# A two-block transformer kernel, its instructions ordered by the other model of time

## The chip, the cores and the metric

One core of one Trainium2 chip. The metric is the device time of one execution in microseconds (us), taken as the median of the runs shown. The engines are PE (TensorE, with its weight loads apart as PEld), DVE (VectorE), ACT (ScalarE), POOL (GpSimd) and SP (SyncE, whose queue here issues all plain loads and stores).

## The reference

Two blocks run one after the other on a sequence of 1024 rows of width 1024, all in fp32. What the change bears on most is cut out here:

```python
def first_block(...):                       # retention part of the mixer
    scores = jnp.einsum('bnihd,bnjhd->bnhij', qc, kc) * decay_in
    y_in = jnp.einsum('bnhij,bnjhe->bnihe', scores, vc)
    kv = jnp.einsum('bnjhd,bnjhe,hj->nbhde', kc, vc, zeta)
...
def second_block(...):
    q, k, v, bg, cg, hv = jnp.split(h @ w_in[l], SPLIT_POINTS, axis=-1)
    att = windowed_attention(q, k, v, k_c, v_c, sink[l])
    conv = short_conv_mixer(bg, cg, hv, conv_w[l])      # bg * conv3(cg * hv)
    x = x + gt1 * (jnp.concatenate([att, conv], axis=-1) @ w_out[l])
    x = x + gt2 * expert_choice_ffn(h2, w_router[l], w_gate[l], w_up[l], w_down[l])
```

Block 1 is a mixer (a 31-tap depthwise convolution beside an 8-head retention in chunks), cross attention over 256 memory rows and a squared-ReLU MLP of width 4096. Block 2 is a windowed attention (8 query heads on 2 key heads; every query sees 256 context keys, the keys at most 128 positions away, and a sink) beside a gated 3-tap convolution, then a mixture of 16 experts, each of which picks its 128 best tokens, and a last norm. A vector of modulations, 6 x 1024 from a matrix of 1024 x 6144, shifts, scales and gates block 2.

## The kernel before

**Products.** Every fp32 product is three matmuls on high and low parts (`mm3`, L139 to L141). Weights come in units of 128x1024 (512 KB, `raw`, L123) and are split by ACT (high part, L114) and DVE (low part, L115) into a ring of five tiles (four during the attention). A block of 128x512 outputs over 1024 inputs is 24 matmuls of 512 columns into one bank of PSUM.

**Order.** The kernel's text issues instructions for one engine after the other; the tile context reorders them before the program is built. It keeps a heap of instructions that are ready, with the position in the text as priority (`tc.high_priority(offset=n)` moves a piece n places ahead), and a model of time that says when an engine and its operands are free. What it writes is one fixed list for each engine, and an engine works through its list in order: an instruction that waits holds back all behind it. The SP queue is such a list too.

**Retention** (block 1, L445 to L524). `retention(t)` is called for 8 tiles of 128 rows: transposes of q and k (`qkT`, L453), copies by ACT (L455, L458), scores (`sc`, L462), decay by DVE, `yin` (L471), copies by ACT (L474), transposes (`yT`, L477), and the state's part (`yx`, L484; `kv`, L499). It is a chain that goes back and forth between PE, ACT and DVE. Later in the text stand the norm and transposes of the convolution's result (`yc` L565, `ptz` L578) and the keys and values of the memory (`km`, `vm`), which depend on nothing of it, then the output product `wo`.

**Attention** (block 2, L926 to L1003). `attention(t)` is called for 8 tiles of 128 queries, t = 0 to 7, and inside for two key heads `kv`, each with four query heads in two pairs:

```python
        p = B(PTB(), "q2T")                                   # L932, transposes L934
        ...
            act.activation(qT[0:64, :, r, :], src, AF.Copy)   # L938, then DVE L939
        ...
                    s2 = ps[0].tile([128, 1024], F32, tag=f"D{jj}", bufs=1, name=nm("s2"))
        ...
                        dve.tensor_reduce(mx, sc, axis=AX.X, op=OP.max)
        ...
                    act.activation(P[:, :256 + nl], sc, AF.Exp, bias=nmx[:, jj:jj + 1], scale=0.125,
        ...
            for kb in range(nkb):
                p = B(PTB(), "P2T")                           # transposes L984
                ...
                evac_split(ph, pl_, p)                        # ACT L201, DVE L202
```

The scores of a head (L956 to L961, five matmuls) go to one of two double banks (D0 and D1, one for each head of a pair); DVE takes the maximum (L964, L966), ACT the exponential (L968) with its row sum. After a pair the row sums are finished (L971 to L975) and P is scaled (L978). Then for each block of 128 keys (five; four in tiles 0 and 7) the four heads' P are transposed into one of two banks (`PTB`), split by ACT and DVE into `P2h` and `P2l`, and multiplied by the values (`o`, L992 to L995). `cor` (L998) and `att` (L1000) close a key head. `q2T` takes a bank of the same pair as the `P2T`.

**Gated convolution** (L1009 to L1037). It stands behind the attention in the text, but depends on nothing of it. For each of four channel groups it has six blocks of 24 matmuls (`cg`, `hv`, `cg`, `hv`, `bg`, `bg`), 24 blocks or 576 matmuls in all, into one bank, read by ACT (L1020) and DVE (L1024, L1035), with the taps on DVE (L1026 to L1028).

**After both** (`mixed`, L1071 to L1117) the attention's and the convolution's results are loaded back from HBM (`mf`), split into `m` (L114, L115, 512 columns) and multiplied by the output weights (`wo`); `lb` (L1054) is a small product ahead of them. Then follow the router, the top-k of 16 rounds on DVE (L1136 to L1139), and the experts.

The change touches `build` alone.

Of the kernel before, what the change touches and what calls it, by code (L numbers as in the profile page):

```python
# [1354 lines left out]
def build(shapes, stop=None, dbg=None):  # L1355
    import concourse.bacc as bacc
    nc = bacc.Bacc("TRN2", target_bir_lowering=False, num_devices=1)
    d = {n: nc.dram_tensor(n, s, dt, kind="ExternalInput").ap() for n, (s, dt) in shapes.items()}
    out = nc.dram_tensor("out_0_dram", (S, D), F32, kind="ExternalOutput").ap()
    dd = {n: nc.dram_tensor(n, s, F32, kind="ExternalOutput").ap() for n, s in (dbg or {}).items()}  # L1360
    with tile.TileContext(nc) as tc:
        tile_kernel(tc, d, out, stop=stop, dbg=dd)
    return nc

# [7 lines left out]
```

## Time and profile before

| what | value |
|---|---|
| median of 3 runs | 2562.68 us (2561.54 to 2565.68) |
| profiled execution, its own time | 2566.32 us |
| its span | 2564.5 us |
| PE, PEld busy | 95%, 77% of the span |
| DVE, ACT, POOL busy | 69%, 45%, 2% |
| mean granted clock of TensorE | 0.979 |
| chain that ended last, by engine | PE 69%, DMA 12%, DVE 12%, ACT 3% |
| HBM traffic | 172 GB/s over the span |

A busy share is a sum over stages with different limits. The chain is followed back from the last instruction to whatever released it. The granted clock has two levels, 1.2 and 2.4 GHz; a PEclk of 1.00 is the upper one all the time, 0.50 the lower. Rows of PE overlap, since matmuls are pipelined: the distance from one start to the next says more than the duration.

### The profile page before, as it was taken

The page shows a single profiled execution, that of the slowest core. Times are in us where ns is not written, and L with a number is a line of the kernel's source. Part 1 is how long each engine was busy: PE and PEld are TensorE (multiplying, and loading weights), DVE is VectorE, ACT ScalarE, POOL GpSimd, SP SyncE. Part 2 cuts the span into 40 slices and gives each one's busy share as a digit, 9 for nine tenths or more (in the row PEclk, how much of TensorE's full clock was granted, in tenths as well). Part 3 has the DMA queues.
Part 4 walks back from the last instruction along what each step waited for, and adds up shares of the span by engine and source line. Part 5 has one row for each costly group of instructions (what it writes and reads, how often), then busy time and mean ns, then how long its engine had stood idle before and what let it go on. Part 6 is the DMA issues. An engine that isn't in the chain of part 4 may idle for free.

```text
span 2564.5 us, 31365 instructions
## 1 busy us (share of the span) xinstructions
PE 2428.0 (95%) x11441; PEld 1968.6 (77%) x11441; DVE 1781.0 (69%) x3158; ACT 1165.1 (45%) x1782; POOL 56.4 (2%) x37
## 2 busy tenths in 40 slices
PE   7999899999999999999999999998983999999995
PEld 6887678888878888888888777776872888888774
DVE  6999883655577555333336758776557999999887
ACT  6113652544442122112215635554332888887775
POOL 0000000000000000000000000000000100011100
PEclk9999999999999999999999999999996999999998
DMA  5233445424443344211112221125672999999994
GB/s 192 86 125 119 162 160 196 141 96 164 135 156 123 124 141 155 65 42 47 58 50 78 91 74 50 38 65 166 209 281 97 385 395 390 391 389 385 359 374 156
DMA packets 138619, 442.85 MB, mean 173 GB/s; under 512 B 15680, under 2 KB 20320, under 8 KB 138464
## 3 DMA queue, kind: packets, MB, share of 16 engines
q1 hardware_dynamic: 133712, 423.54, 46.3%
q0 software_dynamic: 4752, 17.30, 2.7%
q8 instruction: 90, 1.47, 0.2%
q14 instruction: 65, 0.53, 0.1%
HBM read 388.34 MB, written 52.45 MB: 172 GB/s over the span
## 4 chain that ended last, share of the span: by engine, by line
PE 69%; DMA 12%; DVE 12%; ACT 3%; issue 2%; SPq 0%; DVEq 0%; POOLq 0%; ACTq 0%
DMA wada<-w_ada 7%; PE up L140 5%; PE up L141 4%; PE up L139 4%; PE dn L140 4%; PE dn L139 4%; PE dn L141 4%; DVE mws L738 3%; PE wo L140 3%; PE wo L139 3%; PE wo L141 3%; PE ga L140 2%; PE ga L141 2%; PE ga L139 2%; DVE w L115 2%
## 5 line engine op out<-in xcount | busy, mean ns | idle before, releaser
L114 ACT ACTIVATE w<-raw 128x1024 fp32r<-128x1024 f32 x560 | 584.4, 1058 | 754.1 <-PE dn L141 266.8
L115 DVE TENSOR_TENSOR w<-raw,w 128x1024 fp32r<-128x1024 f32 x560 | 674.1, 1223 | 188.7 <-ACT w L114 183.4
L139 PE MATMUL up<-hm,w 128*128 128x512 f32 x512 | 199.6, 390 | 0.0
L139 PE MATMUL dn<-w,uT 128*128 128x512 f32 x512 | 199.4, 390 | 0.1
L140 PE MATMUL up<-hm,w 128*128 128x512 f32 x512 | 199.4, 389 | 0.0
L141 PE MATMUL up<-hm,w 128*128 128x512 f32 x512 | 199.3, 389 | 0.0
L140 PE MATMUL dn<-w,uT 128*128 128x512 f32 x512 | 199.1, 389 | 0.0
L141 PE MATMUL dn<-w,uT 128*128 128x512 f32 x512 | 198.7, 389 | 0.0
L738 DVE CUSTOM_DVE_ANT_0 mws<-wada,crow 128x512 bf16<-128x512 f32 x128 | 88.2, 689 | 105.7 <-DMA wada<-w_ada 103.7
L773 DVE TENSOR_TENSOR acc<-dn,acc 128x512 f32<-128x512 f32 x144 | 97.9, 687 | 91.3 <-PE dn L141 91.0
L395 DVE SCALAR_TENSOR_TENSOR y<-u,small,y 128x1007 f32<-128x1007 f32 (+26 forms) x120 | 146.3, 1263 | 0.5
L139 PEld LDWEIGHTS dn<-w,uT 128*128 128x128 f32 x512 | 96.1, 188 | 20.9 <-DVE uT L758 0.4
L141 PEld LDWEIGHTS dn<-w,uT 128*128 128x128 f32 x512 | 96.0, 188 | 20.6 <-DVE uT L759 0.5
L141 PEld LDWEIGHTS up<-hm,w 128*128 128x128 f32 x512 | 96.1, 188 | 20.1
L139 PEld LDWEIGHTS up<-hm,w 128*128 128x128 f32 x512 | 96.0, 188 | 19.9 <-ACT hm L204 0.3
L140 PEld LDWEIGHTS dn<-w,uT 128*128 128x128 f32 x512 | 96.1, 188 | 19.8
L140 PEld LDWEIGHTS up<-hm,w 128*128 128x128 f32 x512 | 96.1, 188 | 19.7
L140 PE MATMUL ga<-w,x1T 128*128 128x512 f32 x256 | 102.8, 402 | 1.7 <-DVE w L115 1.7
L140 PE MATMUL dn<-w,x1T 128*128 128x512 f32 x256 | 101.6, 397 | 2.0 <-DVE w L115 2.0
L139 PE MATMUL dn<-w,x1T 128*128 128x512 f32 x256 | 102.3, 400 | 0.4 <-ACT w L114 0.4
L141 PE MATMUL ga<-w,x1T 128*128 128x512 f32 x256 | 102.3, 400 | 0.0
L140 PE MATMUL up<-w,x1T 128*128 128x512 f32 x256 | 101.7, 397 | 0.2 <-DVE w L115 0.2
(417 smaller groups left out, 5451.1 us busy)
## 6 DMA issues: line engine op xcount, KB each, us to landing
raw<-experts SPq DMA_DIRECT2D x384, 512.0 KB, 6.8
wada<-w_ada SPq DMA_DIRECT2D x48, 512.0 KB, 3.6
raw<-up_fm SPq DMA_DIRECT2D x32, 512.0 KB, 4.3
raw<-down_tm SPq DMA_DIRECT2D x32, 512.0 KB, 4.4
raw<-w_out_tm SPq DMA_DIRECT2D x24, 512.0 KB, 4.4
raw<-w_in_fm SPq DMA_DIRECT2D x20, 512.0 KB, 3.8
h_d<-hx SPq DMA_DIRECT2D x32, 256.0 KB, 3.0
raw<-xq_fm SPq DMA_DIRECT2D x16, 512.0 KB, 5.2
```

Source lines behind the costliest of these rows:

```text
L114: act.activation(hi, src, AF.Copy)
L115: dve.tensor_sub(lo, src, hi.bitcast(F32))
L139: pe.matmul(out_, l[0], r[0], start=first, stop=False)
L140: pe.matmul(out_, l[0], r[1], start=False, stop=False)
L141: pe.matmul(out_, l[1], r[0], start=False, stop=last)
L395: dve.scalar_tensor_tensor(yc[:, s:], uc[:, :1024 - s], convw[:, c, 30 - s:31 - s], yc[:, s:], op0=OP.mult, op1=OP.add)
L738: dve.tensor_tensor_reduce(out=mjunk, in0=raw[:, h * 512:(h + 1) * 512], in1=crow[o, h], op0=OP.mult, op1=OP.add, scale=1.0, scalar=0.0, a ...
L773: dve.tensor_add(acc[t][:, sl], p, acc[t][:, sl])
```

## The change

One argument of the tile context is set, so that the order of every engine's list is worked out with the context's other model of time, which follows engines and loads on a time line. No instruction is written differently.

```diff
--- before.py
+++ after.py
@@ -1358,7 +1358,7 @@
-    with tile.TileContext(nc) as tc:
+    with tile.TileContext(nc, schedule_with_timeline_sim=True) as tc:
         tile_kernel(tc, d, out, stop=stop, dbg=dd)
```

The two builds have the same instructions, but for loads of ACT's function tables, 45 before and 51 now. Three places where the lists differ are shown: each row is source line, operation, output<-inputs and shape; `x4` stands for four alike. Names are those of the text with a running number.

PE, where attention tile 3 ends and tile 4 begins (`q2T_12989` is tile 4's). Before:

```order
L984 MATMUL P2T_12970<-ident,PW 128x128 x2
L984 MATMUL P2T_12970<-ident,P_2285_12916 128x128
L934 MATMUL q2T_12989<-ident,qt_12986 128x128 x4
L139 MATMUL hv_14262<-hT_1945_11462,w_14172 128x512
L140 MATMUL hv_14262<-hT_1945_11462,w_14172 128x512
L141 MATMUL hv_14262<-hT_1945_11462,w_14172 128x512
L139 MATMUL hv_14262<-hT_1948_11472,w_14172 128x512
L140 MATMUL hv_14262<-hT_1948_11472,w_14172 128x512
L992 MATMUL o_2287_12925<-P2l_12976,V_1880_11058 64x512
L993 MATMUL o_2287_12925<-P2h_12975,V_1880_11058 128x512
L141 MATMUL hv_14262<-hT_1948_11472,w_14172 128x512
L958 MATMUL s_2310_13000<-K_1873_11051,qT_2306_12988 128x384
```

Now:

```order
L984 MATMUL P2T_12970<-ident,P_2285_12916 128x128
L993 MATMUL o_2287_12925<-P2h_12964,V_1879_11057 128x512
L995 MATMUL o_2287_12925<-P2l_12965,V_1879_11057 64x512
L934 MATMUL q2T_12989<-ident,qt_12986 128x128 x4
L992 MATMUL o_2287_12925<-P2l_12976,V_1880_11058 64x512
L993 MATMUL o_2287_12925<-P2h_12975,V_1880_11058 128x512
L958 MATMUL s_2310_13000<-K_1873_11051,qT_2306_12988 128x384
L958 MATMUL s_2310_13000<-K_1874_11052,qT_2306_12988 128x384
L961 MATMUL s_2310_13000<-K2c_11055,qT_2306_12988 128x256 x2
L958 MATMUL s_2313_13011<-K_1873_11051,qT_2306_12988 128x384
L958 MATMUL s_2313_13011<-K_1874_11052,qT_2306_12988 128x384
```

Before, `hv` and `bg` matmuls of the convolution stand between the steps of every attention tile, some three blocks to a tile, and the last five blocks behind the last tile. Now all 24 blocks stand earlier, in runs of 14 to 24 matmuls from the first tile on; the last, `bg_14681`, is issued when the first key head's scores of tile 3 are out. Behind it, in the rest of tile 3 and in tiles 4 to 7, PE's list has attention alone, and `q2T` of a tile stands behind all `P2T` of the one before.

PE, retention tile 6 (`qkT_2443`), with the memory's values `vm`. Before:

```order
L139 MATMUL vm_3202<-w_3184,hP_376 128x512
L453 MATMUL qkT_2443<-ident,qr_2439 128x128 x4
L140 MATMUL vm_3202<-w_3184,hP_376 128x512
L141 MATMUL vm_3202<-w_3184,hP_376 128x512
L139 MATMUL vm_3202<-w_3184,hP_376 128x512
L140 MATMUL vm_3202<-w_3184,hP_376 128x512
L141 MATMUL vm_3202<-w_3184,hP_376 128x512
L139 MATMUL vm_3202<-w_3189,hP_386 128x512
L140 MATMUL vm_3202<-w_3189,hP_386 128x512
L141 MATMUL vm_3202<-w_3189,hP_386 128x512
L139 MATMUL vm_3202<-w_3189,hP_386 128x512
```

Now:

```order
L140 MATMUL vm_3306<-w_3275,hP_406 128x512
L141 MATMUL vm_3306<-w_3275,hP_406 128x512
L453 MATMUL qkT_2443<-ident,qr_2439 128x128 x4
L462 MATMUL sc_2453<-qbd_1396,qkT_1755 128x512
L462 MATMUL sc_2457<-qbd_1396,qkT_1755 128x512
L499 MATMUL kv_2390<-vl_2345,kz_2388 128x256 x2
L471 MATMUL yin_2462<-pf_2455,vl_2441 128x256 x2
L471 MATMUL yin_2467<-pf_2459,vl_2441 128x256 x2
L484 MATMUL yx_2478<-St_1395,qkT_1755 128x256 x2
L477 MATMUL yT_2472<-ident,yF_2461 128x128 x4
```

Before, `vm_3202` and another block stood inside tiles 6 and 7, and `vm_3278` and `vm_3306`, 48 matmuls, behind tile 7. Now all `km` and `vm` blocks stand ahead of tile 6: tiles 6 and 7 and the `ptz` behind them have nothing between, and `wo` follows.

ACT, the splits of the results loaded back (`m`), which `wo` needs. Before they stand together behind the attention:

```order
L114 ACTIVATE m_2659_14742<-mf_14739 128x512
L114 ACTIVATE m_2660_14745<-mf_14739 128x512
L114 ACTIVATE m_2662_14751<-mf_14748 128x512
L114 ACTIVATE m_2663_14754<-mf_14748 128x512
L114 ACTIVATE m_2665_14760<-mf_14757 128x512
L114 ACTIVATE m_2666_14763<-mf_14757 128x512
```

Now those of `mf_14757` and `mf_15237`, which are results of the convolution, stand in tile 5, between the copies of its `q2T` and its first exponentials:

```order
L938 ACTIVATE qT_2378_13243<-q2T_13244 64x4x128
L114 ACTIVATE m_2665_14760<-mf_14757 128x512
L998 ACTIVATE cor_13236<-o_2359_13180 64x512
L114 ACTIVATE m_2666_14763<-mf_14757 128x512
L938 ACTIVATE qT_2378_13243<-q2T_13244 64x4x128
L968 ACTIVATE P_2384_13264,y_13253<-s_2382_13255,y_13254 128x640
L114 ACTIVATE m_2755_15240<-mf_15237 128x512
L114 ACTIVATE m_2756_15243<-mf_15237 128x512
```

The same holds for DVE's half of these splits, and, in tile 6, for those of `mf_14748` (the attention's results of tiles 0 to 3). `m_2659` and `m_2660` stand behind the last tile in both: `mf_14739` lies where the attention keeps a P.

## Rows read from the trace of the kernel before

**Rows 1.** Page, part 1: busy time of each engine (share of the span) and instructions.

```profile
PE 2428.0 (95%) x11441; PEld 1968.6 (77%) x11441; DVE 1781.0 (69%) x3158; ACT 1165.1 (45%) x1782; POOL 56.4 (2%) x37
```

**Rows 2.** Windows: window, us, busy of PE, PEld, DVE, ACT, POOL (x instructions), PEclk, DMA, GB/s.

```profile
1514.60:1798.70 284.10, 272.41 (x1401) 212.22 (x1402) 208.94 (x447) 143.14 (x302) 0.00 (x0) 0.99 0.25 77
...
240.00:350.00 110.00, 100.64 (x511) 77.36 (x511) 94.60 (x306) 59.74 (x124) 0.00 (x0) 0.97 0.46 154
```

**Rows 3.** Groups of instructions, PE, 1514 to 1800 us: count, then busy us, mean ns.

```profile
L139 PE MATMUL cg<-hT,w 128*128 128x512 f32 x64 | 27.0, 422 | 2.8 <-DVE y L1035 1.1 <-ACT K L871 0.9 <-DVE u L1024 0.8
```

**Rows 4.** Timeline, PE: start us, us, instruction.

```profile
1647.33 0.34 PE L956 MATMUL s<-wmr 128*128 128x384 f32 x1
...
1648.08 0.40 PE L141 MATMUL bg<-hT,w 128*128 128x512 f32 x1
...
1651.53 0.39 PE L141 MATMUL bg<-hT,w 128*128 128x512 f32 x1
```

**Rows 5.** Groups of instructions, DVE, 1514 to 1800 us.

```profile
L202 DVE TENSOR_TENSOR P2l<-P2T,P2h 128x512 fp32r<-128x512 f32 x76 | 50.7, 686 | 24.1 <-ACT P2h L201 23.8
...
L964 DVE TENSOR_REDUCE y<-s 128x1 f32<-128x640 f32 x48 | 39.2, 822 | 7.5 <-PE s L961 6.9
...
L978 DVE TENSOR_SCALAR P<-P,y 128x640 f32<-128x640 f32 x30 | 16.0, 548 | 0.2
...
L115 DVE TENSOR_TENSOR w<-raw,w 128x1024 fp32r<-128x1024 f32 x13 | 15.8, 1219 | 7.8 <-ACT w L114 7.8
...
L939 DVE TENSOR_TENSOR qT<-q2T,qT 64x512 fp32r<-64x512 f32 x16 | 11.0, 689 | 11.7 <-ACT qT L938 11.5
...
L1000 DVE TENSOR_TENSOR att<-o,cor 64x512 f32<-64x512 f32 x16 | 10.9, 683 | 6.0 <-ACT cor L998 5.8
...
L966 DVE SCALAR_TENSOR_TENSOR y<-y,nsink 128x1 f32<-128x1 f32 x64 | 9.8, 154 | 0.2
```

**Rows 6.** Groups of instructions, ACT, 1514 to 1800 us.

```profile
L201 ACT ACTIVATE P2h<-P2T 128x512 fp32r<-128x512 f32 x76 | 43.0, 596 | 41.2 <-PE P2T L984 32.4 <-PE o L993 5.4 <-DVE PW L978 1.6
...
L968 ACT ACTIVATE P<-s,y 128x640 f32<-128x640 f32 x30 | 23.8, 795 | 24.0 <-DVE y L966 19.0 <-DVE y L975 5.0
...
L938 ACT ACTIVATE qT<-q2T 64x512 fp32r<-64x512 f32 x16 | 9.5, 592 | 11.1 <-PE q2T L934 7.3 <-DVE qT L939 3.7
...
L968 ACT ACTIVATION_READ_ACCUMULATOR P<-s,y 128x1 f32 x40 | 7.8, 195 | 0.0
```

**Rows 7.** Chain of waits, 1755 to 1800 us: start us, us, what.

```profile
1787.85 5.03 DMA mf<-at
...
1792.96 0.62 ACT m L114
...
1798.71 0.61 PE wo L139
```

**Rows 8.** Chain of waits, 285 to 304 us (retention).

```profile
293.30 0.48 ACT qkT L455
...
300.55 0.22 PE yT L477 x2
```

**Rows 9.** Windows, as rows 2, of 20 us.

```profile
700.00:720.00 20.00, 16.14 (x75) 12.82 (x74) 13.07 (x33) 16.55 (x22) 0.00 (x0) 1.00 0.85 289
...
1415.00:1435.00 20.00, 15.48 (x114) 13.57 (x112) 19.66 (x84) 15.02 (x32) 0.00 (x0) 0.99 0.42 156
```

**Rows 10.** Chain of waits, 1918 to 1970 us (top-k).

```profile
1931.00 1.20 DVE x L193
...
1932.80 1.12 DVE x L1107
```

**Rows 11.** Windows, as rows 2, of 10 us.

```profile
270.00:280.00 10.00, 6.25 (x50) 5.63 (x48) 7.14 (x27) 4.57 (x8) 0.00 (x0) 1.00 0.79 257
...
280.00:290.00 10.00, 9.81 (x43) 7.38 (x44) 7.11 (x23) 3.65 (x9) 0.00 (x0) 0.83 0.36 119
...
1510.00:1520.00 10.00, 6.99 (x23) 5.24 (x24) 2.39 (x8) 3.15 (x14) 0.00 (x0) 0.66 0.49 158
```

## What the change will do: the prediction

> **What bounds the kernel now.** I read the page's busy shares first: TensorE (PE) is busy 95% of the span, VectorE (DVE) 69%, ScalarE (ACT) 45% [rows 1]. So a new order can gain only what PE idles, 5% of the span, and can lose wherever it leaves PE without work. The windows by stage come next, for the two stages in which PE's list changes most. In the attention stretch, 1514.6 to 1798.7 us, PE is busy 272.41 of 284.10 us, DVE 208.94 and ACT 143.14; in the retention's, 240 to 350 us, PE 100.64 of 110 and DVE 94.60 [rows 2]. A reader is to see that PE is nearly full in both although each holds a chain that goes back and forth between engines, and that DVE is not far behind. What fills PE is work of no chain: convolution blocks in the one, memory values in the other. The groups of instructions then give what a chain costs without that filling, and the chain of waits what stands at the seams.
>
> **The change, part by part.** No operation is added or removed but six function-table loads on ACT, an engine that idles 141 us of the attention stretch [rows 2]; I cost them at nothing, and if they fell on a bare chain they would lie within the range.
>
> *Attention stretch, first half (A).* The convolution is 24 blocks of 24 matmuls, 576; the view shows them as nine groups of 64, of which one stands for all [rows 3]. From 1648.08 to 1651.53 us lie 15 intervals, so a matmul takes 3.45/15 = 0.23 us and the convolution 132.5 us [rows 4]. The rest of PE's busy time is the attention and the 3.1 us of `lb`: 272.4 - 132.5 - 3.1 = 136.8 us. Six tiles have five key blocks and two have four; with the short ones at 0.86 that is 7.72 full tiles of 17.7 us on PE. In the new order all of the convolution stands with tiles 0 to 2 and about a fifth of tile 3's PE work: 132.5 + 3.06 x 17.7 = 186.7 us, and some 6 us of idle, about half of what the stretch has now (284.1 - 272.4 = 11.7): **A = 192.7 us**.
>
> *Second half (B): two thirds of tile 3's chain, tiles 4 to 6, and tile 7, 0.67 + 3 + 0.86 = 4.53 tiles with nothing beside them on PE.* The trace shows no bare tile, so I bound one from both sides. Below: DVE alone. Its attention groups (the large ones in [rows 5], with the other shapes of the same lines and the small sums of L971 to L975) add up to 180.7 us, 23.4 per tile. Rows overlap a little at their ends: all of DVE's groups add to 228.2 us where its busy time is 208.94, so the least is 23.4 x 208.94/228.2 = 21.4 us. Above: the chain, step by step. Start of a tile: four transposes, a copy on ACT of 0.59 [rows 6], two subtractions on DVE of 0.69, and three handovers, 3.2 us. Four pairs of heads: a head's scores take 1648.08 - 1647.33 = 0.75 us on PE [rows 4], the maximum 0.82 + 0.15 on DVE [rows 5], the exponential 0.80 + 0.20 on ACT [rows 6], and its bank is free again only then. That is 2.7 us a pair if all else fits beside it, 4.0 if the scaling (two of 0.55) and the splits (0.69) get in its way on DVE: 10.8 to 16. Last sums and scaling, 1.8. Five key blocks over two banks, each with transposes, 0.60 on ACT and 0.69 on DVE, about 1.06 a block: 5.3. What is left of the first key head's blocks: 2. Together 23.1 to 28.3. I take **26 us**, nearer the upper end, since DVE's 21.4 needs DVE never to wait, and in a bare tile it waits at both seams. B = 4.53 x 26 = 117.8 us. Two things are added. ACT and DVE now meet splits of reloaded results in tiles 5 and 6; such a reload took 5.03 us [rows 7], and the chain stands behind it in both engines' lists: 4 us for the part that is not yet in. The first reload `mf_14739` can begin only when tile 7's last P is read; then 5.03 + 0.62 and a subtraction pass before `wo` [rows 7], of which the last `o` and `att` cover a little: 6 us. **B = 127.8 us.**
>
> A + B = 320.5 against 284.1: **+36.4 us**. At 21.4 a tile it is +15.5; at 28.3, +46.8. The tile at which nothing would change is 26 - 36.4/4.53 = 18.0 us, under what DVE needs.
>
> *The clock.* In B, PE has 17.7 us of work in 26. The nearest rows: PE was busy 6.25 us of 270 to 280 at a granted clock of 1.00, and 280 to 290 ran at 0.83; 1510 to 1520 had 6.99 busy at 0.66 [rows 11]. A stretch that pauses like this drops to 1.2 GHz now and then. A window at 0.83 spends a third of itself at the low level and loses some 1.7 us of PE's work, and only matmuls on the chain pass it on; for 12 such windows I take a fifth of 20 us, **+4**, with 0 and 14 as ends.
>
> The Trainium skill (TensorE: Matmul & The Clock Gate, section "A second HAM failure mode: psum-queue depth-cycling") goes further: short idles between groups of matmuls that cycle through PSUM banks are enough to make the clock swing between its levels. By it the sum would be that of the second rival below rather than +4; rows 11 agree that pauses lower the clock, but show it only for single windows.
>
> *Retention.* A tile's chain runs from 293.30 to 300.77 [rows 8], 7.5 us, of which about 4.6 is PE's own work. Tiles 6 and 7 now have no filling: 2 x 2.9 = 5.8 us, and the transposes behind them about 3 more, where 48 `vm` matmuls stood. These fill earlier tiles instead, which idle 9.4 us in this stretch [rows 2]; I count 3 of it back. **+6 us**, ends -3 (all of the idle filled) and +15 (none, and every step bare).
>
> *Gains.* 700 to 720 us idles 3.9 and 1415 to 1435 4.5 us [rows 9]; there the new lists have more matmuls of neighbouring blocks: 1.6 and 2.5 back. Of two row scalings that stand inside the chain of the top-k one is moved ahead of it: 1.20 + 1.12 us [rows 10]. **-6.5 us**, ends 0 and -10. The experts' lists, the MLP's and the cross attention's are nearly as before and cost nothing: PE is full there and stays so.
>
> Sum: 36.4 + 4 + 6 - 6.5 = **+39.9 us** on the profiled execution's 2566.3, 2606.2. That execution lies 3.6 us over the median of the runs, so I forecast **2602 us**.
>
> **Rivals.**
> 1. *Faster: a bare tile runs at PE's pace.* DVE's rows were taken while other work shared its list and PSUM; if they shrink in a bare tile and two tiles' steps overlap, a tile takes 17.7 us. B is then 80.2 + 10 = 90.2, A + B = 282.9, and with the gains and retention at 0 the kernel stands at -1.2 - 6.5 = -7.7, about 2555 us. It decides from 18.0 + 6.5/4.53 = 19.4 us a tile down if clock and retention cost nothing, from 26 - 39.9/4.53 = 17.2 if they cost what I take. For it: PE and not DVE is the full engine now. Against it: DVE's 21.4, and `q2T` behind all `P2T` of the tile before. 0.06.
> 2. *The clock stays at its low level in B.* Then 4.53 x 17.7 = 80.2 us of PE work takes 160.4, and with the 10 us of seams B is 170.4: 42.6 over the 127.8, less the 4 that it replaces, so 2602 + 38.6, about 2641 us. For it rows 11; against it the retention stretch, whose PE pauses too and whose mean is 0.97 [rows 2]. 0.14.
> 3. *DVE packs a bare tile almost fully* (21.4 to 22.5 us), the retention loses nothing and the gains come in full: +15.5 to 20.5, + 0 to 2, - 10: between +5 and +12, 2568 to 2575 us; with a gain overlooked elsewhere it is no change. 0.14, of which 0.05 within 0.2% of before and 0.01 faster.
> 4. *The lists don't decide*, because loads or shared waits set the pace and the stretch's length hardly moves: no row speaks for it, as DMA is at 0.25 there [rows 2]. About 2563 us, 0.04.
>
> My forecast has the remaining 0.62.
>
> **How the numbers follow.** A measurement can tell about 0.2%, 5.1 us, from no change. Faster: rival 1 and 0.01 of rival 3, 0.07. Same: rival 4 and 0.05 of rival 3, 0.09. Slower: 0.84. The range holds the forecast with its ends on tile and clock and reaches into rivals 2 and 3: below to a tile of 22.5 us with the other terms as taken (2602 - 4.53 x 3.5 = 2586) and on to 2572, where rival 3 lies; above to tile 28.3 with the clock at +14, 2602 + 10 + 10 = 2622, and on to 2632, three quarters of the way to rival 2's 2641.
>
> **What would show it.** In the changed kernel's windows, convolution matmuls should end some 190 us into the attention stretch, and the rest be 120 to 135 us with PE near 70%, DVE over 80%. From one `q2T` to the next in tiles 4 to 7 should lie about 26 us. The retention's tiles 6 and 7 should show PE idle behind `sc` and `yT`. I am wrong if tiles 4 to 7 stand under 20 us apart, or if the stretch is as long as before.

## The result and the profile after

| | before | after |
|---|---|---|
| median | 2562.86 us (4 runs) | 2710.21 us (4 runs, 2707.93 to 2715.14) |
| ratio after / before | | 1.0567, 95% interval 1.0553 to 1.0581 |
| profiled execution: own time, span | 2566.32, 2564.5 us | 2709.68, 2707.9 us |
| mean granted clock | 0.979 | 0.961 |

Slower, as forecast, but by 147 us and not by 39; the range ended at 2632 us. Part 1 of the page after, against [rows 1]:

```profile
PE 2465.7 (91%) x11441; PEld 2007.2 (74%) x11441; DVE 1781.9 (66%) x3158; ACT 1178.4 (44%) x1788; POOL 88.1 (3%) x37
```

The same 11441 matmuls. PE's idle time rose from 2564.5 - 2428.0 = 136.5 us to 2707.9 - 2465.7 = 242.2, by 105.7; the other 37.7 us is PE's own busy time, longer for the most part at a lower clock (last section). DVE's busy time hardly changed, 1781.0 and 1781.9 us.

To see where this lies, both spans are cut at the first matmul of a few tiles: `rg` (retention begins), `wo`, `q` (cross attention), `up` (MLP), `modT` (keys, values and queries of block 2), the first `cg` or `s` (attention with the convolution), `lb`, `aT` (router and top-k), `ga` (experts).

| stage, us | before | after | difference | forecast |
|---|---|---|---|---|
| start | 204.4 | 202.7 | -1.7 | 0 |
| retention | 158.8 | 190.2 | **+31.4** | +6 |
| `wo` | 100.6 | 103.2 | +2.6 | 0 |
| cross attention | 242.6 | 256.7 | **+14.1** | 0 (-1.6 at its end) |
| MLP | 705.6 | 734.0 | **+28.4** | 0 |
| keys, values, queries | 102.6 | 101.2 | -1.4 | -2.5 |
| attention | 281.0 | 330.9 | **+49.9** | +36.4, clock +4 |
| second `wo` | 122.4 | 124.4 | +2.0 | 0 |
| top-k | 51.6 | 49.5 | -2.1 | -2.3 |
| experts | 594.9 | 615.1 | **+20.2** | 0 |
| span | 2564.5 | 2707.9 | +143.4 | +39.9 |

Four stages beside the attention lose. The windows of the changed kernel for them, and for the two halves of the attention, A and B (columns as in [rows 2]):

```profile
202.70:392.90 190.20, 153.87 (x725) 117.58 (x724) 151.03 (x405) 82.28 (x162) 0.00 (x0) 0.92 0.40 138
...
496.10:752.80 256.70, 245.77 (x1210) 203.78 (x1208) 129.00 (x262) 121.60 (x212) 0.00 (x0) 0.98 0.38 125
752.80:1486.80 734.00, 709.12 (x3104) 582.53 (x3103) 351.82 (x725) 184.47 (x264) 0.00 (x0) 0.98 0.28 91
...
1588.60:1773.00 184.40, 182.88 (x903) 151.57 (x901) 103.97 (x206) 66.00 (x132) 0.00 (x0) 0.99 0.18 56
1773.00:1918.90 145.90, 102.65 (x484) 74.90 (x482) 106.87 (x239) 75.47 (x166) 0.00 (x0) 0.87 0.25 81
...
2092.80:2707.80 615.00, 571.07 (x2553) 457.45 (x2552) 539.84 (x537) 455.06 (x501) 86.80 (x32) 0.98 0.93 342
```

And of the kernel before, the retention, cross attention, MLP and experts:

```profile
204.40:363.20 158.80, 148.60 (x725) 114.63 (x723) 141.59 (x397) 79.77 (x160) 0.00 (x0) 0.98 0.46 152
...
463.80:706.40 242.60, 240.78 (x1210) 197.80 (x1208) 132.85 (x263) 118.00 (x209) 0.00 (x0) 1.00 0.40 133
706.40:1412.00 705.60, 701.50 (x3103) 578.70 (x3102) 351.23 (x721) 181.33 (x262) 0.00 (x0) 1.00 0.30 94
...
1969.60:2564.40 594.80, 566.18 (x2553) 453.84 (x2552) 538.49 (x537) 451.18 (x501) 55.13 (x32) 0.98 0.94 353
```

In the MLP PE idled 4.1 us of 705.6 before and idles 24.9 of 734.0 now; in the retention 10.2 and 36.3. What it waits for, in the list of PE's waits over the whole span after (us in total, times, longest):

```profile
PE ptz L578 <- DVE z L572: 12.9, 3, 4.8
PE dn L139 <- DVE uT L758: 12.6, 3, 7.6
PE dn L139 <- ACT x1T L201: 9.4, 9, 1.2
PE s L958 <- DVE qT L939: 9.2, 7, 3.3
...
PE yc L565 <- DMA yh<-y: 5.4, 2, 5.2
```

They are from four places of the program, each small: the retention (`ptz`, `yc`), the MLP's `dn`, the experts' `dn`, and the bare attention tiles. The cross attention has no such wait: its idle time grows from 1.8 to 10.9 us, and its largest waits are 3.1 us in sum each (`q` for DVE's `oT`, `PT` for DVE's `P`). Four of the six additional loads of ACT's function tables lie there and two in the MLP, 1.28 us each on ACT.

**Attention.** The last convolution matmul ends A at 1773.0, so A is 184.4 us from the first `cg` (185.0 from the stage's first `s`). The starts of the bare tiles (PE's timeline, `q2T` of tiles 4 to 7):

```profile
1794.74 0.60 PE L934 MATMUL q2T<-ident,qt 128*128 128x128 f32 x4
1823.89 0.60 PE L934 MATMUL q2T<-ident,qt 128*128 128x128 f32 x4
1856.30 0.60 PE L934 MATMUL q2T<-ident,qt 128*128 128x128 f32 x4
1885.83 0.60 PE L934 MATMUL q2T<-ident,qt 128*128 128x128 f32 x4
```

Tiles 4 to 6 take 29.2, 32.4 and 29.5 us, mean 30.4.

**MLP.** The longest wait for `uT`. PE's timeline, then DVE's:

```profile
996.28 0.39 PE L141 MATMUL dn<-w,uT 128*128 128x512 f32 x1
1004.30 0.80 PE L139 MATMUL dn<-w,uT 128*128 128x512 f32 x1 [7.63 <-DVE uT L758]
...
1008.52 0.80 PE L141 MATMUL dn<-w,uT 128*128 128x512 f32 x1 [3.00 <-DVE uT L759]
```

```profile
1000.39 0.69 DVE L738 CUSTOM_DVE_ANT_0 mws<-wada,crow 128x512 bf16<-128x512 f32 x1 [3.67 <-DMA wada<-w_ada]
...
1002.76 0.42 DVE L758 CAST uT<-sq 128x512 fp32r<-128x512 f32 x1
...
1007.78 0.69 DVE L759 TENSOR_TENSOR uT<-sq,uT 128x512 fp32r<-128x512 f32 x1
```

`mws` are the sums for block 2's modulations, work with no hurry that waits for a load. `uT` needs no load, but stands behind it in DVE's list, and PE's next `dn` stands behind `uT`. Before, DVE stood almost as long at these loads in the MLP (103.7 us in its groups, 114.9 now), and yet PE hardly waits in its groups of `dn`: there, as I read it, `uT` was not the next thing PE needed. The first of these groups before:

```profile
L139 PE MATMUL dn<-w,uT 128*128 128x512 f32 x512 | 199.4, 390 | 0.1
```

**Experts.** ACT's timeline after, around one change of expert, then PE's:

```profile
2411.21 1.06 ACT L114 ACTIVATE w<-raw 128x1024 fp32r<-128x1024 f32 x1 [0.30 <-PE dn L141]
2412.17 1.07 ACT L201 ACTIVATE x1T<-pt 128x512 fp32r<-128x512 f32 x2
```

```profile
2411.01 0.60 PE L259 MATMUL pt<-ident,hh 128*128 128x128 f32 x4
2411.44 0.60 PE L259 MATMUL pt<-ident,xs 128*128 128x128 f32 x4
2412.80 0.50 PE L139 MATMUL dn<-w,x1T 128*128 128x512 f32 x1 [0.76 <-ACT x1T L201]
```

Two groups of transposes stand directly behind one another on PE, ACT is still at a weight split, and the `dn` behind them waits for its copy. In PE's list after, ten such groups follow another with no matmul between; in the list before, one.

**Retention.** PE's groups of the retention's window after:

```profile
L484 PE MATMUL yx<-St,qkT 128*128 128x256 f32 x28 | 7.7, 392 | 4.5 <-DVE St L509 3.8 <-ACT qkT L455 0.7
...
L453 PE MATMUL qkT<-ident,qr 128*128 128x128 f32 x32 | 5.8, 313 | 5.0 <-DVE y L516 3.9 <-DVE y L518 1.1
L578 PE MATMUL ptz<-ident,z 128*128 128x128 f32 x12 | 3.3, 435 | 9.5 <-DVE z L572 9.5
L565 PE MATMUL yc<-ident,yh 128*128 128x128 f32 x16 | 3.2, 298 | 5.4 <-DMA yh<-y 5.4
```

The same groups waited 0.0, 0.8, 0.0 and 0.7 us before. These four make 22.9 of the 26.1 us of new idle. Where the first of it arises, PE's timeline and then DVE's:

```profile
271.01 0.69 PE L565 MATMUL yc<-ident,yh 128*128 128x128 f32 x2 [5.21 <-DMA yh<-y]
275.61 1.08 PE L453 MATMUL qkT<-ident,qr 128*128 128x128 f32 x4 [3.91 <-DVE y L516]
```

```profile
265.14 1.87 DVE L521 TENSOR_SCALAR yt<-yt,y,y 128x64 f32<-128x64 f32 x8
...
268.06 0.69 DVE L523 TENSOR_TENSOR yt<-qr,yt 128x512 f32<-128x512 f32 x1
...
274.31 0.69 DVE L487 TENSOR_TENSOR yt<-yT,yx 128x512 f32<-128x512 f32 x1 [4.43 <-DMA yr<-yt]
```

Tile 0's `yt` is finished at 268.06 + 0.69, 38.2 us after its `qkT` (230.59); before, 25.5 us after (227.78 to 252.55 + 0.69). In between DVE's list has 19 taps of the depthwise convolution (L395) and three splits of weights, before 12 taps and no split. Its buffer then goes out by DMA, tile 1's `yt` waits for the buffer, and in PE's list `yc`, which waits for a reload, stands ahead of tile 2's `qkT`. Tiles 0 and 1 take 45.0 us (230.59 to 275.61), and took 30.0 (227.78 to 257.75): half of the stage's loss. By tiles, the windows of tile 1, of tiles 2 to 5 and of tiles 6 and 7 up to `wo`, after and then before:

```profile
248.82:275.61 26.79, 13.32 (x54) 8.64 (x53) 20.44 (x51) 11.10 (x17) 0.00 (x0) 0.87 0.46 156
275.61:358.77 83.16, 77.20 (x408) 61.85 (x409) 59.38 (x195) 46.27 (x87) 0.00 (x0) 0.94 0.43 138
358.77:392.90 34.13, 18.68 (x69) 11.67 (x68) 27.97 (x122) 14.53 (x37) 0.00 (x0) 0.83 0.36 136
```

```profile
237.73:257.75 20.02, 19.65 (x87) 14.97 (x85) 19.21 (x46) 8.45 (x16) 0.00 (x0) 1.00 0.19 65
257.75:324.32 66.57, 58.88 (x333) 46.57 (x333) 54.48 (x191) 38.55 (x78) 0.00 (x0) 0.95 0.52 169
324.32:363.20 38.88, 36.82 (x164) 27.31 (x162) 35.27 (x131) 22.86 (x47) 0.00 (x0) 1.00 0.46 154
```

PE's idle time rises from 0.4 to 13.5 us in tile 1 and from 2.1 to 15.5 in tiles 6 and 7, and falls from 7.7 to 6.0 in tiles 2 to 5.

### The profile page after: what moved, and what is told of

Same layout as the page of the kernel before. It is cut to its first block, busy times and chain, and to the rows that moved or that the text cites. A ratio compares the mean times of both kernels' runs of the same rounds, so it can differ in the third digit from the quotient of the medians.

```text
span 2707.9 us, 31364 instructions
## 1 busy us (share of the span) xinstructions
PE 2465.7 (91%) x11441; PEld 2007.2 (74%) x11441; DVE 1781.9 (66%) x3158; ACT 1178.4 (44%) x1788; POOL 88.1 (3%) x37
## 5 line engine op out<-in xcount | busy, mean ns | idle before, releaser
L139 PE MATMUL dn<-w,uT 128*128 128x512 f32 x512 | 202.2, 395 | 15.7 <-DVE uT L758 12.6
L738 DVE CUSTOM_DVE_ANT_0 mws<-wada,crow 128x512 bf16<-128x512 f32 x128 | 88.3, 690 | 121.0 <-DMA wada<-w_ada 114.9
L395 DVE SCALAR_TENSOR_TENSOR y<-u,small,y 128x1017 f32<-128x1017 f32 (+28 forms) x120 | 145.4, 1261 | 0.3
L139 PEld LDWEIGHTS dn<-w,uT 128*128 128x128 f32 x512 | 97.3, 190 | 38.2 <-DVE uT L758 11.5
L140 PEld LDWEIGHTS dn<-w,uT 128*128 128x128 f32 x512 | 97.4, 190 | 20.2
L139 PE MATMUL ga<-w,x1T 128*128 128x512 f32 x256 | 102.6, 401 | 9.5 <-ACT w L114 5.0
L139 PE MATMUL dn<-w,x1T 128*128 128x512 f32 x256 | 99.4, 398 | 9.4 <-ACT x1T L201 9.4
L140 PE MATMUL up<-w,x1T 128*128 128x512 f32 x256 | 102.8, 402 | 0.0
L139 PE MATMUL up<-w,x1T 128*128 128x512 f32 x256 | 101.1, 395 | 0.0
```

The source lines that it names most:

```text
L139: pe.matmul(out_, l[0], r[0], start=first, stop=False)
L140: pe.matmul(out_, l[0], r[1], start=False, stop=False)
L395: dve.scalar_tensor_tensor(yc[:, s:], uc[:, :1024 - s], convw[:, c, 30 - s:31 - s], yc[:, s:], op0=OP.mult, op1=OP.add)
L738: dve.tensor_tensor_reduce(out=mjunk, in0=raw[:, h * 512:(h + 1) * 512], in1=crow[o, h], op0=OP.mult, op1=OP.add, scale=1.0, scalar=0.0, a ...
```

## Experiments: whole lists put back

Theory 1: a stage loses because PE's filling was moved out of it, so PE's list of before brings it back. Theory 2: it loses because ACT's or DVE's list now meets loads and copies in another order than PE needs them. To tell them apart, the changed model orders the kernel, but the lists of one, two or three engines are tied to what they were before, instruction by instruction:

```diff
+def put_in_order(tc, nc):
+    for name, packed in ORDERS.items():
+        rank = np.frombuffer(zlib.decompress(base64.b85decode(packed)), np.int16)
+        eng = getattr(mybir.EngineType, name)
+        mine = [i for i in nc.cur_bb.bb.instructions if i.engine == eng]
+        seq = [mine[k] for k in rank]
+        for a, b in zip(seq, seq[1:]):
+            tc.add_manual_dep(b, a.name, mybir.DependencyInfo(
+                mybir.DependencyClass.NoSync, mybir.DependencyReason.DATA), reason="order")
...
         tile_kernel(tc, d, out, stop=stop, dbg=dd)
+        put_in_order(tc, nc)
```

`ORDERS` has a table of positions for each engine that is tied. The other engines' lists are the new model's, which fits them to the given ones.

**PE's list.** 

> The other model orders ACT, DVE and the queue, but PE's whole list is held to the order it has in the kernel before. Theory A (the loss is PE's list: filling in whole runs, chains left bare): the attention falls from 331 us (first convolution or score matmul to lb) to 285 to 295, the experts and the MLP stay within 5 us of 615 and 734, and the whole comes to 2640 to 2660. For the retention the runs with its filling held gave nothing back, so there I expect under 10 of the 31 us. Theory B (the lists of ACT and DVE carry the loss everywhere): every stage stays within 10 us of the changed kernel, and the whole over 2690.

**ACT's list.** 

> As the run with PE's list held, but with ACT's list held to its order before instead, PE, DVE and the queue by the other model. The experts decide: there the copies x1T stand one by one between weight splits before, and in clumps of two and three now. If that is what PE waits for, the experts fall from 615 to 595 to 602 us; if they are slower through PE's list or loads, they stay over 610. Attention and retention: within 15 us of the changed kernel by theory A, near the kernel before by theory B.

**DVE's list.** 

> DVE's list alone held to its order before. The MLP decides: there PE waits 15.6 us for uT, which stands behind sums that wait for a load of w_ada. If DVE's list is the cause, the MLP falls from 734 to 706 to 714 us; if the loads' own times are (the queue's order), it stays over 725. The retention's tile goes through a chain on DVE that ends in a store; if DVE's list is the cause there, the retention falls from 190 to under 170.

**The load queue's list** (915 of its 927 instructions). 

> The queue's list alone (915 of its 927 loads and stores) held to the order before. If the order of loads carries the MLP's or the cross attention's loss, these stages fall by 10 us or more each; else no stage moves by more than 8 us, and the whole stays over 2695.

**PE, ACT and DVE.** 

> PE's, ACT's and DVE's lists all held to their order before; only the queue's list is the other model's. If the three lists carry the loss together (single ones held were out of step with the others), every stage comes within 6 us of the kernel before and the whole to 2560 to 2580. If the queue's order of loads carries the MLP's or the cross attention's part, those stages stay 10 us or more over 706 and 243.

**PE and ACT.** 

> PE's and ACT's lists held to the order before, DVE's and the queue's by the other model. If ACT is the partner that PE's list lacks in the MLP (731.9 us with PE's list alone, 709.7 with all three) and the cross attention (270.9 and 245.3), these fall under 716 and 252. If DVE is, they stay over 725 and 260.

**PE and DVE.** 

> PE's and DVE's lists held, ACT's and the queue's by the other model. PE waited in the MLP for uT from DVE, so I expect DVE to be the partner: MLP under 716 us, cross attention under 252. If ACT is, they stay over 725 and 260.

Measured (medians; ratios to the kernel before in the same series; the two pairs ran once):

| lists of before on | time, us | ratio |
|---|---|---|
| none (the change) | 2710.21 | 1.0567 [1.0553, 1.0581] |
| PE | 2653.4 | 1.0354 [1.0324, 1.0384] |
| ACT | 2752.68 | 1.0741 [1.0710, 1.0772] |
| DVE | 2811.71 | 1.0971 [1.0940, 1.1003] |
| load queue | 2743.97 | 1.0707 [1.0676, 1.0738] |
| PE, ACT | 2631.91 | |
| PE, DVE | 2612.68 | |
| PE, ACT, DVE | 2584.31 | 1.0079 [1.0060, 1.0097] |

By stage, in us:

| stage | before | after | PE | ACT | DVE | queue | PE, ACT | PE, DVE | all three |
|---|---|---|---|---|---|---|---|---|---|
| retention | 158.8 | 190.2 | 165.9 | 192.1 | 188.8 | 185.5 | 166.1 | 169.0 | 167.6 |
| cross attention | 242.6 | 256.7 | 270.9 | 267.9 | 287.9 | 265.9 | 249.9 | 257.7 | 245.3 |
| MLP | 705.6 | 734.0 | 731.9 | 729.3 | 725.8 | 749.5 | 729.9 | 709.3 | 709.7 |
| attention | 281.0 | 330.9 | 308.4 | 352.2 | 356.8 | 347.3 | 300.0 | 282.3 | 280.9 |
| experts | 594.9 | 615.1 | 591.5 | 624.2 | 630.1 | 615.4 | 596.2 | 595.6 | 594.1 |

Several expectations missed. PE's list brought the whole to where I had it, but by other stages: the attention stayed over my 295 us, while retention and experts came back by 24 us each, where I had under 10 and at most 5. ACT's list alone did not bring the experts back, DVE's alone neither the MLP nor the retention, and the queue's made cross attention, MLP and attention 9 to 16 us longer. With three lists the whole ended 4 us over my range and the retention 9 us over the kernel before.

Three things follow. PE's list alone restores the experts whole and most of the retention: theory 1 there. In the MLP it restores nothing, but with DVE's it restores 25 of 28 us; in the attention PE's gives 22 of 50 and, with DVE's, 49: theory 2, and of DVE rather than ACT. In the cross attention ACT's list is the better partner for PE's (249.9 us, with DVE's 257.7), and all three are better still. And a list of ACT, DVE or the queue put back *alone* makes the kernel slower than the change did, by 42, 101 and 34 us. I read this as lists that are made to fit one another, one of which, taken from another set, waits for partners that are not there; that reading is argued and not shown. The 21 us that three lists leave over are by stage retention +8.8, second `wo` +5.7, MLP +4.1 and cross attention +2.7. What is still the new model's is above all the queue's list. The first run under "The best of both" has that held too in these stages: the last three are back there (121.1, 706.6 and 242.6 us), the retention is not (166.7), so its 8.8 us stay open.

## Experiments: the filling, stage by stage

**Attention: the convolution spread again.** Each step of three matmuls is held behind a mark in PE's order, the end of `q2T`, of each head's scores or of each key block's transposes, 192 steps over 138 of 148 marks:

```diff
+          with (behind(next(hold)) if hold else nullcontext()):
...
-            fm_block(p, uni[0], half_of(hT2, half))
+            fm_block(p, uni[0], half_of(hT2, half), hold=held)
```

`behind(i)` is `tc.issue_after(i)`: what it encloses is issued behind instruction i.

> The order of the other model, with the convolution's 192 steps of three matmuls held evenly behind the attention's own steps on PE, so that filling stands between the steps of every tile again. Theory (the bare tiles cost it): the stretch from the first convolution matmul to lb, 334 us in the changed kernel against 284 before, falls to 285 to 295, and the whole time by 40 to 48 us, to about 2664. Rival (the loss lies in ACT's and DVE's lists, such as the reloads' splits inside tiles 5 and 6, or in the clock without bare tiles): the stretch stays over 315 and the whole over 2690.

2682.52 us, ratio 1.0464 [1.0446, 1.0481]. The attention takes 304.5 us, 26.4 less than in the change and between the two expectations; its tiles 0 to 6 now take 35.3 to 40.7 us each. Its window:

```profile
1582.90:1887.40 304.50, 270.71 (x1384) 215.77 (x1384) 208.94 (x446) 141.36 (x298) 0.00 (x0) 0.98 0.22 71
```

PE still idles 33.8 us here, against 11.7 in [rows 2]: filling at the right place is half of it; the other half comes back where DVE's list is held beside PE's, as the pair of lists shows.

**Attention: the bare tiles under the model of before.** In the kernel *before*, the convolution's text is moved between tiles 3 and 4, and `q2T` of tiles 4 to 7 is held behind its last matmul:

```diff
+        with (behind(conv_end) if t > 3 else nullcontext()):
...
-    for t in range(8):
+    for t in range(4):
         attention(t)
...
+    conv_end = last_on(PE_)
+    for t in range(4, 8):
+        attention(t)
```

> The kernel before, ordered by its own model, but with the text's convolution ahead of attention tile 4 and q2T of tile 4 held behind all of it, so that tiles 4 to 7 stand bare under the default model's order. If bareness itself sets the 29 to 32 us from one q2T to the next that the changed kernel shows, they stand 28 to 32 us apart here too and the attention takes 315 to 330 us. If the other model's order inside a tile is what is slow, they stand 22 to 26 us apart and it takes 296 to 308.

2645.98 us, ratio 1.0319 [1.0300, 1.0338]. The attention takes 362.1 us, over both expected ranges; all other stages stand within 3 us of before. So the move of the convolution, with nothing else of the change, costs 81 us: 218.6 us lie ahead of tile 4's `q2T`, with some 13 us of PE's idle time, and 143.5 behind it, with the four bare tiles. They stand 37.9, 33.5 and 37.8 us apart, more than the 30.4 in the change: under the new model's order a bare tile is the shorter one, so that having bare tiles, and not their inner order, is what it loses by there. The window over these tiles:

```profile
1734.50:1872.00 137.50, 95.64 (x396) 70.27 (x395) 89.65 (x205) 61.25 (x138) 0.00 (x0) 0.75 0.22 71
```

**Retention: `km` and `vm` held into its tiles.** Marks behind `qkT`, both `sc`, both `yin` and `yT` of each tile; `km` goes over tiles 2 to 5, half of `vm` into tiles 6 and 7, half behind them:

```diff
-            tm_block(p, pair_rhs(memT, rows(j)), uni)
+            tm_block(p, pair_rhs(memT, rows(j)), uni, hold=kv_held)
```

> The order of the other model, with the memory's key and value blocks (km, vm) held behind the steps of retention tiles 2 to 7 and the last two vm blocks behind tile 7. Theory A (tiles 6 and 7 are bare): the stretch from the first retention transposes to wo, 190 us in the changed kernel against 159 before, falls by 10 to 15 us, the rest lying at 250 to 290 us, ahead of these blocks. Theory B (the retention loses by the transposes yc, which stand early in PE's list and wait for a reload): it falls by at most 4 us.

2716.93 us, 1.0590 [1.0573, 1.0608]; retention 191.7 us, nothing back. The windows of tiles 2 to 5 and of tiles 6 and 7:

```profile
275.61:349.96 74.35, 60.10 (x312) 46.98 (x313) 48.93 (x181) 35.90 (x76) 0.00 (x0) 0.87 0.34 115
349.96:394.40 44.44, 38.14 (x169) 29.23 (x169) 37.99 (x136) 26.08 (x50) 0.00 (x0) 0.96 0.50 164
```

The idle time has moved: tiles 6 and 7 idle 6.3 us, 15.5 in the change, but tiles 2 to 5, which have given up blocks for them, idle some 14 us, 6.0 in the change. With the transposes `yc` held as well:

> As the run with km and vm held, and the transposes yc of the convolution's reloaded result held behind retention tiles 3 and later. If the wait of PE for that reload (5.2 us in one piece, with the DVE wait and the chain behind it some 10 us) is a loss of its own, the retention stretch falls by a further 6 to 12 us. If it only hides other idle time, by under 3 us.

2715.49 us, 1.0599 [1.0582, 1.0617]; retention 189.3: 2.4 us less, so that wait for the most part hides other idle time. With the blocks of `rg` for tiles 4 to 7 held four tiles ahead, beside `km` and `vm`:

> The order of the other model, with rg blocks 4 to 7 held behind the steps of retention tiles 0 to 3, and km and vm held behind tiles 2 to 7 as in the earlier run. If the retention lost because its early tiles had spent their filling (rg ahead of tile 0), it falls from 190 us to 165 to 175, as it did with PE's whole list held. If the order of its own steps on PE is what counts, it stays over 183.

2696.63 us in one run; retention 178.4, between the two expectations, 12 of 31 us back. So where `vm` stands does not explain the loss by itself: less filling is left for tiles 1 to 7 (some 197 of the stage's 725 PE instructions are out when tile 1 begins, 145 in the kernel before), and spreading `rg` (the gate, 192 matmuls, of which the change has 168 out when tile 1 begins, this run and the kernel before 120) gives some of it. PE's whole list gives 24 us; which rows of it carry the other 12 stays open.

**Retention: a second place for `yt`.** The buffer that the rows above wait for:

```diff
-        yt = T(5, [128, 8, 64], name="yt")
+        yt = R(31, [128, 8, 64], name="yt") if t in (1, 3, 5) else T(5, [128, 8, 64], name="yt")
```

In the changed kernel: 

> The order of the other model, with a second tile for the retention's result yt in tiles 1, 3 and 5, so that a tile needn't wait for the store of the one before. If that tile and its store set the retention's pace, it falls from 190 us to under 178; if PE's list does, it stays over 185.

2705.87 us in one run; retention 187.9, 2.3 less. Tile 1's `yt` no longer waits, but PE does so at the same place for reloads, `yc` first and then `qkT`:

```profile
273.08 0.69 PE L565 MATMUL yc<-ident,yh 128*128 128x128 f32 x2 [6.44 <-DMA yh<-y]
```

In the kernel before: 

> The same second tile in the kernel before, ordered by its own model. The retention is 158.8 us there with PE busy for 148.6. If the wait for yt is worth anything when filling is there, it falls to 151 to 156 and the whole to 2555 to 2560; else nothing moves by more than 3 us.

2557.80 us, ratio 0.9975 [0.9966, 0.9985]; retention 155.0, 3.8 less. The single buffer is a small price of both kernels, not of the change.

**MLP: no loads for `mws`.** One block of `w_ada` is loaded and used for all 48:

```diff
-            raw = load(R(32, [128, 1024], name="wada"), d["w_ada"][b])
+            raw = wada[0] if wada else load(R(32, [128, 1024], name="wada"), d["w_ada"][b])
```

> The order of the other model; of the 48 blocks of w_ada only the first is loaded and all sums use it, so DVE's sums wait for no load (the other 47 loads are left out). If DVE standing at these loads with uT behind is what PE waits for, the MLP falls from 734 to 706 to 716 us. If it is the norm's reloads at the MLP's start and the clock, it stays over 722.

2696.90 us, 1.0518 [1.0499, 1.0537]; MLP 717.6, between the two ranges, 16.4 of 28.4 us back. PE's group of `dn` in this window, line numbers shifted by three:

```profile
L139 PE MATMUL dn<-w,uT 128*128 128x512 f32 x512 | 200.7, 392 | 7.4 <-DVE acc L776 4.4 <-DVE uT L761 1.8 <-ACT relu L757 1.2
```

The waits for `uT` fall from 12.6 + 3.0 to 1.8 + 0.2 us. PE itself waits for no load in the MLP, with these loads or without. So 16.4 us reach it through DVE's waits for them; what the other 12 go through isn't shown. Both belong to the order: with PE's and DVE's lists of before the MLP takes 709.3 us, and all loads are there.

**Experts: copies ahead of splits on ACT.** From the timeline above I first took ACT's list for the cause: a split of the next weights stands ahead of `x1T`. So the splits of `ud` and of the next expert's `ua` are held behind `x1T`:

```diff
-                ud = wunits(d["experts"], e * 24 + 16 + kp * 4 + nb * 2, 2)
+                with behind(hmarks[kp]):
+                    ud = wunits(d["experts"], e * 24 + 16 + kp * 4 + nb * 2, 2)
```

> The order of the other model, with ACT's splits of an expert's down units held behind the copies x1T of its hidden values, and those of the next expert's first units behind that expert's gathered x1T. Theory (x1T stands behind splits that wait for PE to free a weight tile): PE's waits for x1T and for ACT's split in the experts, 19.9 us in sum against about 0.4 of that kind before, fall under 5 us and the experts' stretch from 615 to 597 to 602 us. Rival (the experts are slower through loads or the clock): no change within 4 us.

2720.50 us, 1.0609 [1.0591, 1.0627]; experts 625.9, worse by 10.8. PE waits 9.7 us for the late splits instead:

```profile
L151 PE MATMUL dn<-w,x1T 128*128 128x512 f32 x256 | 102.9, 402 | 9.7 <-DVE w L116 9.7
```

With ACT's whole list of before the experts take 624.2, with PE's 591.5. My theory of ACT's list fell. The releaser that the profile names, ACT, copies transposes that PE has bunched, and bunches grew here: 16 groups follow another with no matmul between, ten in the change, one with PE's list. But bunches are not all of it, for with ACT's list there are three and with DVE's one, and the experts take 624.2 and 630.1 us. Shown is that PE's list, with the others fitted to it, brings the stage back.

**The best of both.** First, lists of before for each stage in which they won, the new model's for the rest, and the experts' lists from the run with PE's list:

> All four lists held to the order before in the retention, the output product, the cross attention, the MLP, the attention and the product behind it; the other model's own order in the start, the keys' and queries' stage and the top-k, where it measured 1.7, 1.4 and 2.1 us shorter; in the experts the lists of the run with PE held, 3.4 us shorter. If stages keep their times when they are put together: 2552 to 2558 us, under both kernels. If the seams between stages cost it back: 2560 to 2575.

2574.01 us, 1.0045 [1.0029, 1.0061], slower than before: against the kernel before its retention is 7.9 us longer, its attention 4.2 and its first `wo` 3.4, and the other stages together give half of that back. Then the other way, the model of before everywhere, with the second `yt` and those experts' lists:

> The kernel before with the retention's second tile yt, ordered by its own model but in the experts, where all four lists are those of the run with PE's list held (591.5 us there against 594.9). If they keep that: 2553 to 2557 us, under the 2557.8 of the second tile alone. If not, 2556 to 2561.

2556.65 us, **0.9968 [0.9956, 0.9981]**, the fastest of all. Against the second `yt` alone (2557.80) the intervals overlap, so that the experts' lists add anything is not shown.

## Why the prediction was wrong in size

Spans differ by 143.4 us where 39.9 were forecast. The 103.5 between them, step by step:

1. **"The experts', MLP's and cross attention's lists are nearly as before and cost nothing: PE is full there and stays so": +62.7 us.** This is the step that failed. I read that PE was full, and did not ask what kept it full. Shifts of the lists against one another were enough for 14.1, 28.4 and 20.2 us, by single waits of up to 7.6 us. The lists could be compared ahead of the run: `uT` against `mws` on DVE, the bunched transposes on PE, though the experts' runs leave open how much these bunches cost. The six additional loads of function tables, which I had at nothing, lie in two of these stages; with three lists put back they are gone, and what they cost apart from the order isn't shown.
2. **Retention, forecast +6, ends -3 and +15, measured +31.4.** Tiles 6 and 7 went bare as I said, and PE idles 15.5 us there: some 6 at the tiles' own steps, where I had 5.8, but 9.5 ahead of `ptz`, which waits for DVE's `z`, where I had about 3. Against before it is 13.4 us for my 8.8. Tiles 2 to 5 give back 1.7 us of the 3 that I counted. The term that I lacked is tile 1, 13.1 us: DVE's list finishes tile 0's `yt` 13 us later, `yc` stands ahead of tile 2's `qkT`, and most of the `rg` that filled PE there is spent. Which of these decides isn't settled: PE's list put back gives 24 us, DVE's alone 1.4, `rg` spread 12. PE's busy time, at a granted clock of 0.92 against 0.98, adds 5.3.
3. **Attention, forecast 36.4 + 4, measured 49.9.** The bare tiles are where it lies, so the mechanism was right, but not all of it: filling spread again gave 26.4 us back, and the rest needed DVE's list, for which I had only the 4 us at the reloads. A is 184.4, not 192.7: with filling PE idles 1.5 us there, not 6. The mis-sized term is the bare tile. I took 26 us between ends of 21.4 and 28.3, and the clock apart; spread over 4.53 tiles the clock's 4 us makes 26.9, and the row is 30.4. Then B is 4.53 x 30.4 = 137.7 us and 8.2 are left of its 145.9 for the seams up to `lb`, or 11.6 up to `wo` (1922.3), where I had 10. PE is busy 70% in B, as forecast, but by luck: 17.7 us of work in 30.4 is 58%, and longer rows make up the rest. DVE is busy 73%, not over 80%, so DVE waits too, and the tile lasts longer than the chain of waits that I added up at 23.1 to 28.3.
4. **Clock.** B's granted clock is 0.87, and PE's busy time there is 102.65 us for the 4.53 x 17.7 = 80.2 us that I counted, 22.4 more. Not all of that is the clock: by the trace's clock records PE is busy 29.8 us of B at the lower level, and half of it, 14.9 us, is an estimate of what the clock takes, against the 20 that I had. That a fifth of it reaches the chain can't be told from these runs. The second rival, the low level throughout, did not come: its 2641 us lies nearer to the result than my forecast, but for the wrong reason. The Trainium skill (TensorE: Matmul & The Clock Gate, "A second HAM failure mode: psum-queue depth-cycling") says that short idles between groups of matmuls made the clock swing in a kernel that cycles through PSUM banks. B's 0.87 agrees: a swing, not a fall for good. The section doesn't speak of a clock that stays low, so that the second rival's sum, which I gave for it, does not follow from it.
5. **Gains, forecast -6.5.** The top-k gives 2.1 (forecast 2.3). 1415 to 1435, now in a stage of 101.2 us, gives 1.4 (2.5). 700 to 720 lies at the edge of a stage that lost 14.1, and nothing of it can be seen. The start gave 1.7 that I had not seen.

Steps 1 to 3 make 62.7 + 25.4 + 9.5 = 97.6; the two `wo` stages (+4.6) and gains short by 1.3 make the rest. The first rival (faster, by PE's pace) and the third (DVE packs a bare tile) are excluded by 30.4 us a tile, and the fourth (the lists don't decide) by the run with three lists.

## What to carry to other kernels

The engine at 95% was full here because the other engines' lists handed it each tile in time; before a new order is costed at nothing in a stage, look in that stage at what stands directly ahead of each result that the full engine reads, on the engine that makes it. An in-order list can't be judged apart from its partners: taken from another set one at a time, three of four made things worse. And filling is a fixed amount: put into a bare stretch, it bares the one that it came from. Last, the releaser that a wait names may itself be late for the sake of the waiting engine's own order: try both lists before either is blamed.

## What the runs showed of the hardware

One pause is paid more than once. After the wait of 7.63 us in the MLP (above) the windows of PE read:

```profile
990.00:996.00 6.00, 6.00 (x28) 4.99 (x27) 3.45 (x10) 1.12 (x2) 0.00 (x0) 1.00 0.40 135
996.00:1004.30 8.30, 0.67 (x4) 0.21 (x3) 4.54 (x11) 2.36 (x4) 0.00 (x0) 0.68 0.32 94
1004.30:1008.00 3.70, 1.22 (x2) 0.50 (x2) 0.84 (x3) 0.33 (x1) 0.00 (x0) 0.50 0.54 214
1008.00:1012.00 4.00, 3.48 (x8) 2.80 (x9) 2.21 (x4) 0.00 (x0) 0.00 (x0) 0.50 0.45 132
1012.00:1016.00 4.00, 4.00 (x17) 3.20 (x17) 2.90 (x8) 0.00 (x0) 0.00 (x0) 0.92 0.34 132
```

The granted clock falls during the pause and stands at 0.50, 1.2 GHz, while work is there again: from 1008 to 1012 us PE is nearly full and runs 8 matmuls, from 1012 to 1016 17. Over the kernel, by the clock records of the two traces, PE is busy 34.8 us at the lower level before and 104.4 now. Half of the difference, 34.8 us, is an estimate of what the clock adds to the busy time of the same matmuls, near the 37.7 us measured. It is a quarter of the difference between the spans; how much of it the span would get back isn't shown. I had 4 us, in one stage.

The same busy share went with two clocks: in B and in the bare tiles under the model of before, PE is busy 70% (102.65 of 145.9 and 95.64 of 137.5 us), and the granted clock is 0.87 in the one and 0.75 in the other.
